# The feed-forwards' first products as seven products of quarters in a two-layer hybrid encoder

## The chip, the core and the metric

The kernel runs on one core of a Trainium2 chip. A core has five engines, each with its own queue that it works off in order: TensorE (PE, matrix products into PSUM), VectorE (DVE), ScalarE (ACT), GpSimd (POOL) and SyncE (SP, which only starts transfers here). The metric is the device time of one launch in microseconds (us).

## The reference

512 frames and 16 learned meta tokens go through a layer norm and two layers. The model has 1024 channels, a feed-forward has 2752 hidden columns in each of its two column sets.

```python
def swiglu_ffn(x, w13, w2):
    a, u = jnp.split(x @ w13, 2, axis=-1)
    return (jax.nn.silu(a) * u) @ w2
...
    for l in range(DEPTH):
        h = layer_norm(DEEPNORM_ALPHA * h + 0.5 * swiglu_ffn(h, ffn1_w13[l], ffn1_w2[l]), ln_g[l, 0], ln_b[l, 0])
        mix = token_mix(h, w_in[l], ...)
        h = layer_norm(DEEPNORM_ALPHA * h + mix, ln_g[l, 1], ln_b[l, 1])
        h = layer_norm(DEEPNORM_ALPHA * h + 0.5 * swiglu_ffn(h, ffn2_w13[l], ffn2_w2[l]), ln_g[l, 2], ln_b[l, 2])
    return h[:, N_META:]
```

`token_mix` is a projection, three groups of heads (trailing means, a depthwise convolution, chunked retention) and an output projection. All is float32.

## The kernel before

**Layout.** Activations lie transposed, channels on the 128 partitions, tokens along the columns, in 8 row tiles. The tokens are cut into two halves, s = 0 and 1, each of 256 frames and 8 meta tokens (264 columns; 256 in the last feed-forward, which drops the meta tokens). Tile m of half s is `h[m][s]`.

**Precision.** The matmuls' operands are of type float32r. Each float32 operand is split into `hi` (rounded to it, a ScalarE cast) and `lo` (the rest, a VectorE subtraction), and `mm3` makes a product of three matmuls, hi·hi, hi·lo and lo·hi, into the same PSUM bank. `xs[m][s]` is the pair for `h[m][s]`. Weights come by transfer into a raw slot of 128 x 1024 (`RAW` of them), are cast as a whole and subtracted in pieces of 512 columns into `hi` and `lo` slots (`WB` of each).

**Stages.** f0a, m0, f0b, f1a, m1, f1b: each layer l has a feed-forward a, a mixer m and a feed-forward b.

**A feed-forward** (`ffn`; the last is `last_ffn`). The hidden columns are cut into 21 units of 128 (of a and of u) and a half unit, numbered 21, with 64 of each. `PARTS` groups the units; for each part, `hidden_part` makes the hidden activations (a unit's first product by `project`: 8 row tiles times a and u times 3 matmuls for each half, `hidden` then gates and splits them), and eight steps, one for each output row tile m and each half, multiply them by `w2` (weights named `o<part>_<m>`) and add the result to h. In part 0 the first `AHEAD` = 3 units are done for half 0 first, then for half 1, since half 1's norm ends later.

**The seam to the next stage.** In the last part `normed` sets the order of the steps so that half 0 is finished first: its statistics (`center`: a mean by a matmul with ones, squares on ScalarE, a variance by a matmul, its root on VectorE, a matmul that spreads it) run beside the last `SKEW` = 6 steps of half 1, and half 1's statistics beside the next stage's first products.

**What sets the order.** The program is written as calls; a scheduler places the instructions on each engine's queue by the order of issue and the dependences, and `issue_after` holds a group back until a named instruction (`rooted["first"]` and `["second"]` are the ends of the two roots of the seam before). The kernel names 8 PSUM banks: 4 `acc`, 2 `att`, 2 `stat`.

## Time and profile before

| | before |
|---|---|
| median of 3 runs | 2049.79 us (2049.25 to 2050.43) |
| the profiled execution: own time, span | 2050.98 us, 2049.2 us |
| stages f0a, m0, f0b, f1a, m1, f1b end at | 386, 630, 1016, 1402, 1643, 2049 us |
| TensorE busy, matmuls | 98%, 15344 |
| VectorE, ScalarE, GpSimd busy | 52%, 31%, 9% |

The profile is of one execution. A row of a timeline is a start, a length and an instruction; successive rows of one engine overlap (a matmul's row of 264 columns is 0.28 us long and the next starts 0.12 us after it), so the spacing from start to start says what one costs in a run. Line numbers are those of the kernel before.

### The profile page before, as it was taken

The page shows a single profiled execution, that of the slowest core. Times are in us where ns is not written, and L with a number is a line of the kernel's source. Part 1 is how long each engine was busy: PE and PEld are TensorE (multiplying, and loading weights), DVE is VectorE, ACT ScalarE, POOL GpSimd, SP SyncE. Part 2 cuts the span into 40 slices and gives each one's busy share as a digit, 9 for nine tenths or more (in the row PEclk, how much of TensorE's full clock was granted, in tenths as well). Part 3 has the DMA queues.
Part 4 walks back from the last instruction along what each step waited for, and adds up shares of the span by engine and source line. Part 5 has one row for each costly group of instructions (what it writes and reads, how often), then busy time and mean ns, then how long its engine had stood idle before and what let it go on. Part 6 is the DMA issues. An engine that isn't in the chain of part 4 may idle for free.

```text
span 2049.2 us, 36659 instructions
## 1 busy us (share of the span) xinstructions
PE 2001.1 (98%) x15344; PEld 1924.7 (94%) x15344; DVE 1055.9 (52%) x2450; ACT 643.4 (31%) x1180; POOL 194.1 (9%) x283
## 2 busy tenths in 40 slices
...
GB/s 150 132 113 85 99 87 83 74 92 80 63 41 43 97 119 95 93 87 90 64 96 89 101 95 94 89 87 75 71 90 63 42 64 102 96 101 102 84 103 42
DMA packets 54118, 177.98 MB, mean 87 GB/s; under 512 B 6192, under 2 KB 10160, under 8 KB 53952
## 3 DMA queue, kind: packets, MB, share of 16 engines
...
q10 hardware_dynamic: 1152, 1.05, 0.2%
q14 instruction: 46, 0.38, 0.1%
...
## 4 chain that ended last, share of the span: by engine, by line
PE 84%; DVE 9%; POOL 2%; issue 2%; ACT 1%; DVEq 0%; POOLq 0%; ACTq 0%
PE f1a_y L104 2%; PE f0a_y L104 2%; PE f1a_y L105 2%; PE f1bo L764 2%; PE f1bo L766 2%; PE f0a_y L105 2%; PE f1bo L765 2%; PE f0a_y L103 2%; PE f1a_y L103 2%; PE f0b_y L104 2%; PE f0b_y L105 2%; PE f0b_y L103 2%; DVE m0y L486 1%; DVE m1y L486 1%; PE m1o L614 1%
## 5 line engine op out<-in xcount | busy, mean ns | idle before, releaser
L92 DVE TENSOR_TENSOR f1bw_l<-f1bw_r,f1bw_h 128x512 fp32r<-128x512 f32 x42 | 27.9, 685 | 48.0 <-ACT f1bw_h L89 48.0
L92 DVE TENSOR_TENSOR f0b_o_l<-f0b_o_r,f0b_o_h 128x512 fp32r<-128x512 f32 (+1 forms) x48 | 28.6, 618 | 45.1 <-ACT f0b_o_h L89 45.1
L92 DVE TENSOR_TENSOR f1a_o_l<-f1a_o_r,f1a_o_h 128x512 fp32r<-128x512 f32 (+1 forms) x48 | 28.7, 620 | 45.0 <-ACT f1a_o_h L89 45.0
L92 DVE TENSOR_TENSOR f0a_o_l<-f0a_o_r,f0a_o_h 128x512 fp32r<-128x512 f32 (+1 forms) x48 | 28.6, 618 | 44.8 <-ACT f0a_o_h L89 44.8
L486 DVE SCALAR_TENSOR_TENSOR m1y<-m1u,vec,m1y 128x528 f32<-128x528 f32 x60 | 46.7, 814 | 0.1
L486 DVE SCALAR_TENSOR_TENSOR m0y<-m0u,vec,m0y 128x528 f32<-128x528 f32 x60 | 46.6, 814 | 0.1
L89 ACT CAST f0b_o_h<-f0b_o_r 128x1024 fp32r<-128x1024 f32 (+1 forms) x24 | 22.5, 939 | 55.1 <-PE f0b_y L104 15.6
L89 ACT CAST f1a_o_h<-f1a_o_r 128x1024 fp32r<-128x1024 f32 (+1 forms) x24 | 22.5, 939 | 54.9 <-PE f1a_y L104 15.6
L89 ACT CAST f0a_o_h<-f0a_o_r 128x1024 fp32r<-128x1024 f32 (+1 forms) x24 | 22.5, 938 | 54.7 <-PE f0a_y L104 15.6
L825 POOL TENSOR_TENSOR yt<-yt,g_last 128x256 f32<-128x256 f32 x4 | 3.1, 782 | 346.8 <-ACT yt L824 346.8
L89 ACT CAST f1bw_h<-f1bw_r 128x1024 fp32r<-128x1024 f32 (+1 forms) x22 | 22.2, 1007 | 43.8 <-PE f1bo L766 6.9
L308 DVE TENSOR_TENSOR h<-h,f0b_y 128x264 f32<-128x264 f32 x32 | 13.7, 428 | 41.9 <-PE f0b_y L105 41.9
L308 DVE TENSOR_TENSOR x<-x,f0a_y 128x264 f32<-128x264 f32 x32 | 13.7, 428 | 41.7 <-PE f0a_y L105 41.6
L308 DVE TENSOR_TENSOR h<-h,f1a_y 128x264 f32<-128x264 f32 x32 | 13.7, 427 | 41.7 <-PE f1a_y L105 41.5
L251 POOL TENSOR_TENSOR f0b_ln_s<-h,h 128x264 f32<-128x264 f32 x2 | 1.5, 752 | 324.7 <-DVE h L308 324.7
L251 POOL TENSOR_TENSOR f1a_ln_s<-h,h 128x264 f32<-128x264 f32 x2 | 1.5, 754 | 324.1 <-DVE h L308 324.1
L251 POOL TENSOR_TENSOR f0a_ln_s<-x,x 128x264 f32<-128x264 f32 x2 | 1.5, 758 | 322.3 <-DVE x L308 322.3
L770 DVE TENSOR_TENSOR yt<-yt,f1bo 128x256 f32<-128x256 f32 x48 | 17.2, 417 | 24.8 <-PE f1bo L766 24.8
L104 PE MATMUL m0mo<-m0cat_l,m0wo_h 128*128 128x264 f32 x96 | 27.7, 290 | 0.0
L104 PE MATMUL m1mo<-m1cat_l,m1wo_h 128*128 128x256 f32 x96 | 27.6, 288 | 0.0
L103 PE MATMUL m0mo<-m0cat_h,m0wo_h 128*128 128x264 f32 x96 | 27.4, 288 | 0.0
L105 PE MATMUL m0mo<-m0cat_h,m0wo_l 128*128 128x264 f32 x96 | 27.3, 285 | 0.0
...
## 6 DMA issues: line engine op xcount, KB each, us to landing
f1bw_r<-in_w2last SPq DMA_DIRECT2D x20, 512.0 KB, 4.3
f0a_o_r<-in_w SPq DMA_DIRECT2D x16, 512.0 KB, 4.3
f0b_o_r<-in_w SPq DMA_DIRECT2D x16, 512.0 KB, 3.8
f1a_o_r<-in_w SPq DMA_DIRECT2D x16, 512.0 KB, 4.0
m0wo_r<-in_w_out SPq DMA_DIRECT2D x8, 512.0 KB, 3.5
m1wo_r<-in_w_out SPq DMA_DIRECT2D x8, 512.0 KB, 3.5
m0w_r<-in_w_in SPq DMA_DIRECT2D x6, 512.0 KB, 3.6
m1w_r<-in_w_in SPq DMA_DIRECT2D x6, 512.0 KB, 3.6
```

The costliest lines, as they stand in the source:

```text
L89: nc.scalar.copy(out=hi[:, :n], in_=w[:, :n])
L92: e.tensor_tensor(out=lo[:, sl], in0=w[:, sl], in1=raw(hi[:, sl]), op=ALU.subtract)
L103: nc.tensor.matmul(out, lhsT=wh, rhs=xh, start=start, stop=False)
L104: nc.tensor.matmul(out, lhsT=wh, rhs=xl, start=False, stop=False)
L105: nc.tensor.matmul(out, lhsT=wl, rhs=xh, start=False, stop=stop)
L308: nc.vector.tensor_tensor(out=y, in0=y, in1=ps, op=ALU.add)
L486: nc.vector.scalar_tensor_tensor(out=ys[c], in0=src, scalar=wk, in1=ys[c], op0=ALU.mult, op1=ALU.add)
L614: nc.tensor.matmul(o[:, c0 : c0 + cw], lhsT=v, rhs=sm, start=i == 0, stop=i == len(sms) - 1)
L764: nc.tensor.matmul(o, lhsT=hh, rhs=wh, start=part > 0 and i == 0, stop=False)
L765: nc.tensor.matmul(o, lhsT=hh, rhs=wl, start=False, stop=False)
L766: nc.tensor.matmul(o, lhsT=hl, rhs=wh, start=False, stop=i == nk - 1)
L770: nc.vector.tensor_tensor(out=y[:, :256], in0=y[:, :256], in1=o, op=ALU.add)
```

## The change

Units 0, 1 and 21 of each feed-forward are made as before. For each of the other 19, the two column sets of a unit (a, u), the two halves of the rows of the weights (row tiles 0 to 3 and 4 to 7) and the two halves of the tokens form a 2 x 2 by 2 x 2 block product. It is made with Winograd's form of Strassen's method: seven products of quarters in place of eight, of sums of the operands.

- `sums`, once in a feed-forward, makes s1 to s4 of `h` (16 sums on VectorE) and splits them (16 casts, 16 subtractions) into wide slots.
- `sum_weights`, for each unit, makes t1 to t4 out of the raw weights, in place, and splits them: on VectorE four sums and seven subtractions of 512 columns, on ScalarE two casts of 1024 and three of 512.
- `hidden_by_sums` issues the products in the order P, R, P, Q, P, Q, P, where P, Q and R are banks. A bank is added to over several products; between them ScalarE copies what it holds (m1, u2, m5, u3), and VectorE forms a and u of both halves of the tokens from the copies.
- Five parts in place of three, four to five units each. `RAW` is 4 in place of 3, `WB` 5 in place of 7, `hc` (the ring of split hidden tiles) 20 in place of 32. `SKEW_F` = 8 holds for the seams behind feed-forwards: all steps of half 0 come before any of half 1.
- A pool of 16 wide slots of 558 columns holds what had slots of its own: the tokens at the start, sequences and windows of the mixer, its last split heads, the last `w2` and `w_out` weights (`weights_wide`), and the split sums.
- The norm behind the mixer keeps h for all tiles, which `sums` needs.

```diff
-TILES = {"x": 32, "h": 16, "hc": 32, "g": 4, "r2": 2, "sm": 5, "s": 2, "q": 4, "dg": 2}
+TILES = {"x": 32, "h": 16, "hc": 20, "g": 4, "r2": 2, "sm": 5, "s": 2, "q": 4, "dg": 2}
+WIDE, WIDES = 558, 16
 BANKS = {"acc": 4, "att": 2, "stat": 2}
-RAW, WB = 3, 7
-SKEW, AHEAD = 6, 3
+RAW, WB, YB = 4, 5, 2
+SKEW, SKEW_F, AHEAD = 6, 8, 3
 
...
-PARTS = ([0, 1, 21, 2, 3, 4], list(range(5, 13)), list(range(13, 21)))
+PARTS = ([0, 1, 21, 2, 3], *(list(range(u, u + 4)) for u in (4, 8, 12)), list(range(16, 21)))
...
+    def wide(name, dt=F32):
+        return sq_pool.tile([P, WIDE], dt, tag="wide", name=name, bufs=WIDES)
...
-    def normed(n, step, ns, v, name, keep):
+    def normed(n, step, ns, v, name, keep, skew):
 
         for s in range(2):
-            for m in range(n - SKEW):
+            for m in range(n - skew):
                 step(m, s)
-        for m in range(n - SKEW, n):
+        for m in range(n - skew, n):
             step(m, 0)
...
+    def sums(n, name):
+        out = [[], [], [], []]
+        for i in range(KT // 2):
+            (a11, a21), (a12, a22) = ([y[:, :n] for y in h[m]] for m in (i, i + KT // 2))
+            s1, s2, s3, s4 = (t(f"{name}s{j}{i}", "q" if i % 2 else "sm")[:, :n] for j in range(4))
+            nc.vector.tensor_tensor(out=s1, in0=a21, in1=a22, op=ALU.subtract)
+            nc.vector.tensor_tensor(out=s2, in0=s1, in1=a11, op=ALU.subtract)
+            nc.vector.tensor_tensor(out=s3, in0=a11, in1=a21, op=ALU.subtract)
+            nc.vector.tensor_tensor(out=s4, in0=a12, in1=s2, op=ALU.add)
+            for j, y in enumerate((s1, s2, s3, s4)):
+                out[j].append(split_wide(y, n, f"{name}S{j}{i}"))
+        return out
+    def half_split(w, hi, lo, c):
+        sl = slice(c, c + 512)
+        nc.scalar.copy(out=hi[:, sl], in_=w)
+        nc.vector.tensor_tensor(out=lo[:, sl], in0=w, in1=raw(hi[:, sl]), op=ALU.subtract)
+    def sum_weights(src, name):
+        def pair(k, w=1024, b=WB):
+            return [wp.tile([P, w], F32R, tag=f"{p_}{'' if w == 1024 else w}", name=f"{name}{k}_{p_}", bufs=b) for p_ in ("hi", "lo")]
+        wa, wu = (wp.tile([P, 1024], F32, tag="raw", name=f"{name}{b}_r", bufs=RAW) for b in "au")
+        nc.sync.dma_start(out=wa, in_=src[0])
+        nc.sync.dma_start(out=wu, in_=src[1])
+        b11, b21, b12, b22 = wa[:, :512], wa[:, 512:], wu[:, :512], wu[:, 512:]
+        add = lambda o, y: nc.vector.tensor_tensor(out=o, in0=o, in1=y, op=ALU.add)
+        A, X, U, Y = pair("a"), pair("x"), pair("u"), pair("y", 512, YB)
+        nc.scalar.copy(out=A[0], in_=wa)
+        for c in (0, 512):
+            nc.vector.tensor_tensor(out=A[1][:, c : c + 512], in0=wa[:, c : c + 512], in1=raw(A[0][:, c : c + 512]), op=ALU.subtract)
+        add(b11, b12)
+        half_split(b11, *X, 0)
+        add(b12, b22)
+        nc.scalar.copy(out=U[0], in_=wu)
+        add(b11, b22)
+        half_split(b11, *X, 512)
+        for c in (0, 512):
+            nc.vector.tensor_tensor(out=U[1][:, c : c + 512], in0=wu[:, c : c + 512], in1=raw(U[0][:, c : c + 512]), op=ALU.subtract)
+        add(b21, b11)
+        half_split(b21, *Y, 0)
+        return [at(w, slice(c, c + 512)) for w, c in ((A, 0), (A, 512), (X, 0), (X, 512), (U, 0), (U, 512), (Y, 0))]
+    def hidden_by_sums(w, S, n, name):
+        b11, b21, t1, t2, t3, b22, t4 = w
+        s1, s2, s3, s4 = S
+        a11, a12, a22 = ([xs[m][s] for m in range(k, k + KT // 2)] for k, s in ((0, 0), (KT // 2, 0), (KT // 2, 1)))
+        p_, q_, r_ = acc(f"{name}P"), acc(f"{name}Q"), acc(f"{name}R", "att")
+        def product(o, x, w, first):
+            for i in range(KT // 2):
+                mm3(o[:, :n], at(w, slice(i * P, (i + 1) * P)), at(x[i], slice(0, n)), first and i == 0, i == KT // 2 - 1, True)
+        def copy(o, k):
+            y = t(f"{name}{k}", "sm")[:, :n]
+            nc.scalar.copy(out=y, in_=o[:, :n])
+            return y
+        def gated(g, u, s):
+            nc.vector.scalar_tensor_tensor(out=g, in0=u, scalar=0.5, in1=g, op0=ALU.mult, op1=ALU.mult)
+            return split(g, n, f"{name}x{s}")
+        product(p_, a11, b11, True)
+        m1 = copy(p_, "m1")
+        product(r_, a12, b21, True)
+        nc.vector.tensor_tensor(out=m1, in0=r_[:, :n], in1=m1, op=ALU.add)
+        g0 = t(f"{name}g0", "g")[:, :n]
+        nc.scalar.activation(g0, m1, AF.Silu)
+        product(p_, s2, t2, False)
+        u2 = copy(p_, "u2")
+        product(q_, s1, t1, True)
+        m5 = copy(q_, "m5")
+        product(p_, s3, t3, False)
+        u3 = copy(p_, "u3")
+        nc.vector.tensor_tensor(out=m5, in0=m5, in1=u3, op=ALU.subtract)
+        product(q_, s4, b22, False)
+        nc.vector.tensor_tensor(out=u2, in0=q_[:, :n], in1=u2, op=ALU.subtract)
+        first = gated(g0, u2, 0)
+        product(p_, a22, t4, False)
+        g1 = t(f"{name}g1", "g")[:, :n]
+        nc.scalar.activation(g1, p_[:, :n], AF.Silu)
+        return [first, gated(g1, m5, 1)]
+    summed = {}
     def hidden_part(part, src, ns, name, between={}):
         hid, w = {}, {}
-        for u, s in in_two(PARTS[part], AHEAD if part == 0 else 0, between):
+        plain = PARTS[part][: AHEAD if part == 0 else 0]
+        for u, s in in_two(plain, AHEAD, between):
             if s == 0:
-                i = PARTS[part].index(u)
-                late = part == 0 and "first" in rooted and i >= LATE_W
+                i = plain.index(u)
+                late = "first" in rooted and i >= LATE_W
                 with tc.issue_after(rooted["second" if i >= LATE_B else "first"]) if late else nullcontext():
                     w[u] = unit_weights(u, src, f"{name}_{u}")
                 hid[u] = []
             hid[u].append(hidden(u, w[u], s, ns[s], f"{name}_{u}"))
+        if part == 0:
+            summed[name] = sums(ns[0], name)
+        for u in PARTS[part][len(plain) :]:
+            with tc.issue_after(rooted["second"]) if plain and "second" in rooted else nullcontext():
+                wu = sum_weights(src["p"][u], f"{name}_{u}")
+            hid[u] = hidden_by_sums(wu, summed[name], ns[0], f"{name}_{u}")
         return hid
...
-                    w[m] = weights(w2[m, :, full[0] * P : (full[0] + nk) * P], nk * P, f"{name}_o{part}_{m}")
+                    make = weights_wide if part == len(PARTS) - 1 and m >= KT - 3 else weights
+                    w[m] = make(w2[m, :, full[0] * P : (full[0] + nk) * P], nk * P, f"{name}_o{part}_{m}")
...
-                normed(KT, step, ns, v, f"{name}_ln", i == 1)
+                normed(KT, step, ns, v, f"{name}_ln", i == 1, SKEW_F)
...
-                w[m] = weights(a["w_out"][l, m], 1024, f"{name}wo{m}")
+                w[m] = (weights_wide if m >= KT - 2 else weights)(a["w_out"][l, m], 1024, f"{name}wo{m}")
...
-        normed(KT, step, no, V_LN + (3 * l + 1) * 16, f"{name}_ln", not last)
+        normed(KT, step, no, V_LN + (3 * l + 1) * 16, f"{name}_ln", True, SKEW)
```

Three places show how the instructions stand.

VectorE's queue in f1a, from the last of the splits of the sums to the first product of unit 2 (`f1aS` is a split sum, `f1a_2a_lo` and `f1a_2x_lo` are subtractions for unit 2's weights, line 427 its sums of weights, `f1a_21h` the gate of the half unit, `f1a_2m` what comes out of unit 2's first two banks). After the change:

```order
L127 TENSOR_TENSOR f1aS_13084<-f1as_13070,f1aS_13084 128x264 [waits Activation_49]
L390 SCALAR_TENSOR_TENSOR f1a_21h_12998<-f1a_21p_0_12972,f1a_21g_12997 64x264 [waits PE_49,Activation_49]
L390 SCALAR_TENSOR_TENSOR f1a_21h_12998<-f1a_21p_0_12972,f1a_21g_12997 64x264
L431 TENSOR_TENSOR f1a_2a_lo<-f1a_2a_r,f1a_2a_hi 128x512 [waits DMAHW2_49]
L117 TENSOR_TENSOR f1a_21x_l<-f1a_21h_12998,f1a_21x_h 128x264 [waits Activation_49]
L431 TENSOR_TENSOR f1a_2a_lo<-f1a_2a_r,f1a_2a_hi 128x512
L427 TENSOR_TENSOR f1a_2a_r<-f1a_2a_r,f1a_2u_r 128x512 [waits DMAHW3_49,DVE_49]
L427 TENSOR_TENSOR f1a_2u_r<-f1a_2u_r 128x512 [waits DVE_49]
L416 TENSOR_TENSOR f1a_2x_lo<-f1a_2a_r,f1a_2x_hi 128x512 [waits Activation_49]
L468 TENSOR_TENSOR f1a_2m_13130<-f1a_2R,f1a_2m_13130 128x264 [waits PE_49]
```

Before, the same gate of the half unit stands behind unit 2's weights and the last split of the norm:

```order
L92 TENSOR_TENSOR f1a_2u_l<-f1a_2u_r,f1a_2u_h 128x512 [waits DMAHW1_49]
L92 TENSOR_TENSOR f1a_2u_l<-f1a_2u_r,f1a_2u_h 128x512
L291 TENSOR_TENSOR f0b_ln_x6l<-h_1_7281,f0b_ln_x6h 128x264 [waits Activation_49]
L363 SCALAR_TENSOR_TENSOR f1a_21h_11921<-f1a_21p_0_11895,f1a_21g_11920 64x264 [waits PE_49,Activation_49]
L363 SCALAR_TENSOR_TENSOR f1a_21h_11921<-f1a_21p_0_11895,f1a_21g_11920 64x264
L98 TENSOR_TENSOR f1a_21x_l<-f1a_21h_11921,f1a_21x_h 128x264 [waits Activation_49]
```

The weights of unit 2, which stood ahead of the half unit's gate, now stand behind it and behind all sums.

ScalarE's queue in f1a, in the middle of part 1 (line 458 copies a bank, 415 casts a sum of weights, 429 and 435 cast raw weights, 470 is a silu). After the change:

```order
L458 COPY f1a_4m_13722<-f1a_4P 128x264 [waits PE_49]
L415 CAST f1a_5x_hi<-f1a_5a_r 128x512 [waits DVE_49]
L435 CAST f1a_5u_hi<-f1a_5u_r 128x1024 [waits DVE_49,DMAHW3_49,PE_49,Activation_49]
L470 ACTIVATE f1a_4g_13737<-f1a_4m_13722 128x264 [waits DVE_49]
L458 COPY f1a_4u_13751<-f1a_4P 128x264 [waits PE_49]
L415 CAST f1a_5x_hi<-f1a_5a_r 128x512 [waits DVE_49]
L429 CAST f1a_6a_hi<-f1a_6a_r 128x1024 [waits DMAHW4_49,PE_49,Activation_49]
L458 COPY f1a_4m_13765<-f1a_4Q 128x264 [waits PE_49]
L458 COPY f1a_4u_13779<-f1a_4P 128x264 [waits PE_49]
```

Before, at the same place:

```order
L368 ACTIVATE f1a_5g_12895<-f1a_5p_0_12845 128x264 [waits PE_49]
L97 CAST f1a_5x_h<-f1a_5g_12895 128x264 [waits DVE_49]
L89 CAST f1a_8u_h<-f1a_8u_r 128x1024 [waits DMAHW7_49,PE_49,Activation_49]
L368 ACTIVATE f1a_5g_12952<-f1a_5p_0_12902 128x264 [waits PE_49]
L89 CAST f1a_9a_h<-f1a_9a_r 128x1024 [waits DMAHW0_49,PE_49,Activation_49]
L97 CAST f1a_5x_h<-f1a_5g_12952 128x264 [waits DVE_49]
```

Between two reads of PSUM there stood at most one cast of weights; now the copies of a unit's banks stand among up to two, one of them waiting for VectorE, and weights are made one to two units ahead instead of three to four.

ScalarE's queue at the seam from f0b to f1a (line 291, before 264, is the square of a centred tile; `f1a_0a`, `f1a_0u` are the next stage's first weights). After the change:

```order
L116 CAST f0b_20x_h<-f0b_20g_12108 128x264 [waits DVE_49]
L104 CAST f0b_o_7_h_12295<-f0b_o_7_r 128x128
L291 ACTIVATE f0b_ln_q_12327<-h_0_7236 128x264 [waits DVE_49]
L91 CAST f1a_0a_h<-f1a_0a_r 128x1024 [waits DMAHW5_49,PE_49]
L291 ACTIVATE f0b_ln_q_12330<-h_0_7271 128x264 [waits DVE_49]
L291 ACTIVATE f0b_ln_q_12334<-h_0_7340 128x264 [waits DVE_49]
```

Before:

```order
L97 CAST f0b_20x_h<-f0b_20g_11045 128x264 [waits DVE_49]
L89 CAST f0b_o_7_h<-f0b_o_7_r 128x1024 [waits DMAHW2_49,PE_49]
L89 CAST f1a_0a_h<-f1a_0a_r 128x1024 [waits DMAHW3_49,PE_49]
L264 ACTIVATE f0b_ln_q_11379<-h_0_6775 128x264 [waits DVE_49]
L264 ACTIVATE f0b_ln_q_11382<-h_0_6810 128x264 [waits DVE_49]
```

The cast of `f1a_0a`, which stood ahead of the first square, stands between the first and the second.

## Rows read from the trace of the kernel before

**Rows 1.** The page: span, busy time by engine, the chain that ended last.
```profile
span 2049.2 us, 36659 instructions
PE 2001.1 (98%) x15344; PEld 1924.7 (94%) x15344; DVE 1055.9 (52%) x2450; ACT 643.4 (31%) x1180; POOL 194.1 (9%) x283
...
PE 84%; DVE 9%; POOL 2%; issue 2%; ACT 1%; DVEq 0%; POOLq 0%; ACTq 0%
```

**Rows 2.** Windows: length, busy us of each engine, PEclk, DMA share, GB/s.
```profile
752.00:860.00 108.00, 108.00 (x887) 108.00 (x886) 39.19 (x77) 30.53 (x52) 0.00 (x0) 1.00 0.32 95
860.00:915.00 55.00, 55.00 (x453) 55.00 (x452) 17.83 (x34) 10.51 (x14) 0.00 (x0) 1.00 0.30 87
1016.00:1402.00 386.00, 383.08 (x3128) 381.08 (x3126) 164.85 (x348) 117.79 (x207) 20.98 (x26) 1.00 0.31 89
```

**Rows 3.** TensorE's waits at the seam f0b to f1a: total us, times, longest.
```profile
PE f0b_ln_rs L159 <- DVE f0b_ln_q L271: 1.0, 1, 1.0
...
PE f1a_0p L104 <- DVE f0b_ln_x6l L291: 0.8, 1, 0.8
...
PE f0b_ln_rs L171 <- DVE f0b_ln_dg L162: 0.4, 1, 0.4
...
PE f0b_ln_mean L256 <- DVE f0b_ln_s L254: 0.3, 1, 0.3
PE f1a_0p L104 <- DVE f0b_ln_x4l L291: 0.3, 1, 0.3
```

**Rows 4.** TensorE's timeline, first and last of 96 matmuls, f0b and f1b.
```profile
798.32 0.28 PE L103 MATMUL f0b_9p<-m_ln_x0h,f0b_9a_h 128*128 128x264 f32 x1
...
809.92 0.28 PE L105 MATMUL f0b_9p<-m_ln_x7h,f0b_9u_l 128*128 128x264 f32 x1
...
1811.35 0.28 PE L103 MATMUL f1b_9p<-m_ln_x0h,f1b_9a_h 128*128 128x256 f32 x1
...
1822.51 0.28 PE L105 MATMUL f1b_9p<-m_ln_x7h,f1b_9u_l 128*128 128x256 f32 x1
```

**Rows 5.** TensorE's timeline at the seam f0b to f1a.
```profile
1016.40 0.71 PE L256 MATMUL f0b_ln_mean<-f0b_ln_s,ones 128*128 128x264 f32 x2
...
1036.21 0.28 PE L103 MATMUL f1a_0p<-f0b_ln_x0h,f1a_0a_h 128*128 128x264 f32 x1
...
1059.66 0.39 PE L104 MATMUL f1a_0p<-f0b_ln_x6l,f1a_0a_h 128*128 128x264 f32 x1 [0.77 <-DVE f0b_ln_x6l L291]
```

**Rows 6.** VectorE's timeline: weights of unit 6; the seam f0b to f1a.
```profile
739.96 1.29 DVE L92 TENSOR_TENSOR f0b_6a_l<-f0b_6a_r,f0b_6a_h 128x512 fp32r<-128x512 f32 x2 [0.33 <-ACT f0b_6a_h L89]
...
1033.42 0.43 DVE L291 TENSOR_TENSOR f0b_ln_x0l<-h,f0b_ln_x0h 128x264 fp32r<-128x264 f32 x1
...
1038.80 2.81 DVE L262 TENSOR_TENSOR h<-h,f0b_ln_mean 128x264 f32<-128x264 f32 x8 [0.81 <-PE f0b_ln_mean L256]
...
1049.33 2.08 DVE L281 SCALAR_TENSOR_TENSOR h<-h,vec,f0b_ln_rs 128x264 f32<-128x264 f32 x5
...
1058.63 0.97 DVE L291 TENSOR_TENSOR f0b_ln_x6l<-h,f0b_ln_x6h 128x264 fp32r<-128x264 f32 x1
1059.63 0.88 DVE L363 SCALAR_TENSOR_TENSOR f1a_21h<-f1a_21p,f1a_21g 64x264 f32<-64x264 f32 x2
```

**Rows 7.** ScalarE's timeline in f0b: weight casts, a silu, a cast.
```profile
774.61 1.05 ACT L89 CAST f0b_9u_h<-f0b_9u_r 128x1024 fp32r<-128x1024 f32 x1 [4.48 <-PE f0b_6p L104]
775.57 0.38 ACT L368 ACTIVATE f0b_6g<-f0b_6p 128x264 f32<-128x264 f32 x1
775.85 1.04 ACT L89 CAST f0b_10a_h<-f0b_10a_r 128x1024 fp32r<-128x1024 f32 x1
776.79 0.41 ACT L97 CAST f0b_6x_h<-f0b_6g 128x264 fp32r<-128x264 f32 x1
```

**Rows 8.** The page's DMA issues: count, KB each, us to landing.
```profile
f1a_o_r<-in_w SPq DMA_DIRECT2D x16, 512.0 KB, 4.0
```

More of the change, by code (lines that the diff above doesn't have):

```diff
@@ L93, in weights, with weights_wide, tile_of @@
         return hi, lo
+    def weights_wide(src, n, name):
+        w = wp.tile([P, 1024], F32, tag="raw", name=f"{name}_r", bufs=RAW)
+        nc.sync.dma_start(out=w[:, :n], in_=src)
+        out = []
+        for c in range(0, n, 512):
+            k = min(512, n - c)
+            hi, lo = (wide(f"{name}_{p_}{c}", F32R) for p_ in "hl")
+            nc.scalar.copy(out=hi[:, :k], in_=w[:, c : c + k])
+            nc.vector.tensor_tensor(out=lo[:, :k], in0=w[:, c : c + k], in1=raw(hi[:, :k]), op=ALU.subtract)
+            out.append((hi, lo))
+        return out
+    def tile_of(w, j):
+        if isinstance(w, list):
+            return at(w[j // 4], slice(j % 4 * P, (j % 4 + 1) * P))
+        return at(w, slice(j * P, (j + 1) * P))
     def split(src, n, name, tag="hc"):
```

52 lines of the change are left out of this document (28 added, 24 removed).

## The prediction, made before the changed kernel was run

> **What bounds the kernel now.** The page comes first. TensorE is busy 98% of the span and the chain that ended last runs 84% on it [rows 1]: VectorE at 52% and ScalarE at 31% are covered. The shares are averages, so the stages come next. The windows [rows 2] show a whole feed-forward (1016 to 1402 us) with TensorE at 383.08 of 386 us and full clock; a stretch of first products alone (752 to 860) and one of second products alone (860 to 915) have TensorE busy all the time, VectorE 36% and 32%, ScalarE 28% and 19%. In the list of TensorE's waits every one of a feed-forward lies at its seam to the next stage; the five of the seam from f0b to f1a [rows 3] add up to 2.8 us. So inside a feed-forward the time is the number of matmuls times their spacing, and what is taken from that number comes off the time as long as nobody else is late.
>
> **What the change removes.** A unit of 128 hidden columns costs 96 matmuls for both halves before (2 halves, 2 column sets, 8 row tiles, 3 matmuls) and 84 after (7 products, 4 row tiles, 3 matmuls). Units 0, 1 and the half unit 21 stay plain, so 19 units in each of four feed-forwards lose 12 matmuls: 684 of 264 columns in three of them, 228 of 256 columns in the last. Their spacing is read from start to start over one half of unit 9 [rows 4]: (809.92 − 798.32)/95 = 122.1 ns at 264 columns, (1822.51 − 1811.35)/95 = 117.5 ns at 256. 684 × 0.1221 + 228 × 0.1175 = 83.5 + 26.8 = **110.3 us off**. The second products keep their matmuls; five parts in place of three only group them differently.
> The Trainium skill ("TensorE: Matmul & The Clock Gate", section "Back-to-back issue gap") gives columns/2.4 GHz + 2.5 ns for the gap of warm matmuls, 112.5 and 109.2 ns here, with which the gain would be 101.8 us; it speaks of an isolated gap. The rows include the weight load of each matmul, and the measurement decides.
>
> **What it adds off the path.** Prices from rows: a 512-column VectorE pass 0.61 us apiece in a run ([rows 6], two in 1.29 with an overlap), a 264-column pass 0.35 (eight in 2.81), a 1024-column ScalarE cast 1.05, a 264-column pass out of PSUM 0.38, a cast of 264 0.41 [rows 7]; a 512-column cast is not in the rows, between the last two by length 0.62 (estimate). A sum unit needs on VectorE 11 passes of 512 and 7 of 264 (before 4 and 4): 11 × 0.61 + 7 × 0.35 = 9.2 us. On ScalarE two casts of 1024, three of 512, four copies out of PSUM, two silus, two casts of 264: 2.1 + 1.9 + 1.5 + 0.8 + 0.8 = 7.1 us. TensorE's unit is 84 × 0.122 = 10.25 us. Both fit, VectorE with 1 us to spare. A part's second product (8 steps of two halves, 24 matmuls, 23 us) asks VectorE for about 16 × 0.35 + 8 × 0.61 = 11 us, so a backlog of a part is worked off there. The cover is thus thin but closed, and I price the averages at nothing; without it each microsecond of VectorE over 10.25 in a unit costs 76 us. SyncE's queue moves the same bytes through four raw slots instead of three: a unit's two transfers wait for the last pass over the unit two ahead, land 4.0 us later [rows 8] and have a whole unit's 10.25 us for it: nothing, unless VectorE is over 6 us late. The other edits (wide slots for tokens, mixer sequences and some weights, h kept by the mixer norm) fall where [rows 1] show VectorE half idle: nothing, ±3 us.
>
> **What it adds on the path.**
> *(a) The first sum unit of each feed-forward.* Its operands are sums over h of both halves, so it needs the second half's norm in full. At the seam the spread of the second half starts on VectorE at Z = 1049.33 [rows 6], and TensorE, after waiting for the last lo tile (x6l), resumes at 1059.66 = Z + 10.3 [rows 5]. About 80 plain matmuls are left there by the order, so they end at Z + 10.3 + 9.8 = Z + 20.1. VectorE has from x6l on 16 sums and 16 splits, 32 × 0.35 = 11.2 us, 12 with a few waits for casts: Z + 22.4. The first place shown from the order says what stands behind them in VectorE's queue: the two gates of the half unit (0.88 us [rows 6]) and a 512 pass of unit 2's weights (0.62), and only then can the first lo matmul run; four hi matmuls (0.5 us) can run ahead. That is 22.4 + 1.5 − 0.5 − 20.1 = 3.3 us of stall. The unit's other weights are made behind it, at 0.61 us a pass and some products need two or three passes while the one before lasts 1.46: I put 0.4 for t1, 1.2 for t2, 0.5 for the next unit's first piece, 2 us. And the part's first second-product weights wait for a raw slot that unit 3 frees only with its last pass, and then stand on ScalarE ahead of a bank copy: about 2 us. Together 7 us for three feed-forwards, 5 for the first (its second half enters early): **26**, bounds 8 (2 each, part of the 3.3 alone) and 50 (VectorE 12 us late each time, as if nothing of the sums were covered).
> *(b) The seams.* The feed-forward norms now do all eight steps of the first half before any of the second. Between the first half's mean and the next stage's first use lie 1036.21 − 1016.40 = 19.8 us now [rows 5], and the chain of that norm ends with x0l on VectorE at 1033.42 + 0.43 [rows 6], 17.4 us after the mean. After the change the order has 111 matmuls there, 13.6 us, and 0.85 for the statistics' own matmuls: 14.4 us. ScalarE's queue (the third place) has a 1024 cast of the next stage's weights between the first two squares of the chain, where it stood ahead of both. So the chain comes out about 3 us late, where the first half waits 1.0 + 0.4 us on the variance and its root today [rows 3]: about 2 us more at three seams, **6**, bounds 0 (VectorE freer, chain 14 us) and 15.
> *(c) Bank handshakes.* No row of before shows a bank read while the next product waits to go on in it. Here ScalarE copies m1, u2, m5 and u3 out of two banks, and TensorE is back in a bank after one other product, 12 × 0.122 = 1.46 us. A copy (0.38) fits, and one that stands right behind a 1024 cast (1.05 + 0.38 = 1.43, the second place shown) just about. 45 of the 76 copies of m5 stand so. I take 0.1 us for each of these: **5**, bounds 0 and 25 (the copy a whole 0.38 late with a hand-over as long as the 0.3 to 0.4 us waits in [rows 3]).
> *(d) Into each second product*, the last unit's lo split is about 0.35 us late, some 16 times: **5**, bounds 0 and 10.
>
> **Sum.** The profiled execution took 2050.98 us, 1.2 above the median of the runs. 2050.98 − 110.3 + 26 + 6 + 5 + 5 = 1982.7, less 1.2: **1981 us**.
>
> **The rivals.**
> *Everything hidden.* The sums start as the spread goes and the handshakes all fit; then 2050 − 110 plus 1 to 15 us, about **1945**. For it: ScalarE 30% and VectorE 43% busy over the feed-forward [rows 2]. Against it: the 12 us of sums have one engine and stand in one place of its queue.
> *Banks decide.* Each unit loses about 0.7 us because two of the four copies stand behind a cast that itself waits for data: 76 × 0.7 = 53 us more than full gain on top of (a) and (b), about **2030**. For it: casts in the order wait for a DMA and for VectorE, and everything behind waits too. Against it: they are made a unit ahead. The Trainium skill ("PSUM — Partial Sum Buffer", section "🎯 Summary: rules for kernel authors") says to read PSUM beside a running matmul only in another bank and to guard by bank, so each of these waits is unavoidable; no run here shows yet what one costs.
> *VectorE becomes the bound, slower.* A unit saves 12 × 0.122 = 1.46 us. If VectorE, with its waits for TensorE and ScalarE inside the unit, takes over 10.25 + 1.46 = 11.7 us for it instead of 9.2, the change loses on each of 76 units; at 12.5 us it is (12.5 − 11.7) × 76 = 61 us slower, less what second products work off, plus (a) and (b): about **2100**. For it: 18 passes in strict order, most of which wait for a cast of ScalarE or for a product. Against it: weights are made a unit ahead, and when VectorE is late its waits vanish, so it goes back to 9.2.
> *No change:* losses of about 110 us, an accident between the last two.
>
> **How the numbers follow.** Forecast (1958 to 2008) 0.60; everything hidden 0.13; banks decide (2008 to 2045) 0.16; no change 0.03; slower 0.08. Within 0.2%, about 4 us, a measurement of this kernel can't tell from no change. Faster is 0.60 + 0.13 + 0.16 = 0.89, same 0.03, slower 0.08. The range leaves out the lower half of the second case, the upper half of the third, and the last two, about 0.2: 1948 to 2022.
>
> **What would show it.** TensorE's instructions about 14,420 instead of 15,344, with spacing unchanged in a sum unit. (a): a TensorE wait of about 3 us on VectorE's unit-2 weights in each feed-forward, then one on o0_1. (b): the waits on x0l and the variance grow at three seams. (c): waits of 0.1 to 0.2 us on the copies, in about half of the units. VectorE busy near 1580 us; inside a hidden stretch near 90%. The prediction is wrong if TensorE's waits in the middle of parts (units 5 to 20) sum to much over 15 us, or if the first sum unit starts without a stall.

## The result, and the profile after

The changed kernel takes 1979.93 us (median of 4 runs, 1979.15 to 1982.23), the kernel before 2049.52 on the same chip (2048.08 to 2050.43): a ratio of 0.9663, with an interval of 0.9646 to 0.968. It is 3.4% faster. The forecast was 1981 us, with 1948 to 2022 as the range.

The page of the changed kernel answers to [rows 1]:

```profile
span 1977.5 us, 36739 instructions
...
PE 1912.4 (97%) x14423; PEld 1826.3 (92%) x14423; DVE 1548.9 (78%) x3466; ACT 920.1 (47%) x1845; POOL 215.0 (11%) x283
...
PE 79%; DVE 12%; POOL 3%; issue 3%; ACT 2%; DMA 0%; SPq 0%; DVEq 0%; POOLq 0%; ACTq 0%
```

TensorE has 921 instructions fewer (912 of them in the units) and is still busy nearly all the time, although VectorE went from 52% to 78%. The chain that ended last has more of VectorE in it (12% after 9%): somewhere it now sets the time. The windows say where not. The first is the whole of f1a, the second its units 4 to 7, the third the second product behind them (columns as in [rows 2]):

```profile
997.47:1366.78 369.31, 361.27 (x2897) 356.29 (x2897) 288.33 (x603) 186.47 (x376) 24.93 (x32) 1.00 0.30 94
1085.74:1126.95 41.21, 41.21 (x338) 41.03 (x337) 33.09 (x64) 24.15 (x49) 0.00 (x0) 1.00 0.32 98
1126.95:1150.63 23.68, 23.68 (x194) 23.53 (x193) 17.44 (x36) 7.79 (x12) 0.00 (x0) 1.00 0.34 102
```

Inside a part TensorE is never without work: it is busy 41.21 of 41.21 us, with VectorE at 80% and ScalarE at 59% beside it. But f1a as a whole has 8.0 us in which TensorE is not busy, where it had 2.9 before in [rows 2]. The list of TensorE's waits for that stretch, from its last norm matmuls on (total us, times, longest), shows one that is new:

```profile
PE f1a_2P L135 <- DVE f1a_2a_lo L431: 2.5, 1, 2.5
PE f0b_ln_rs L201 <- DVE f0b_ln_dg L192: 0.7, 1, 0.7
PE f1a_0p L133 <- ACT f0b_ln_x0h L315: 0.4, 1, 0.4
```

It is the first sum unit. The other feed-forwards have it too: 1.1 us in f0a and 2.8 in f0b on the same subtraction, and 3.1 in f1b on ScalarE's cast of that unit's sum of weights.

The balance of the two profiled executions: the span fell by 2049.2 − 1977.5 = 71.7 us, and 684 matmuls of 122.1 ns and 228 of 117.5 ns are worth 110.3, so 38.6 us were given back (the medians are 69.6 us apart, so single executions leave some 2 us open):

| where | predicted, us | found, us |
|---|---|---|
| (a) start of the sums, four times | 26 | 22.2 (25.6 against the same parts without sums) |
| (b) seams, three | 6 | 6.5 |
| (c) hand-overs of banks | 5 | 6.6 |
| (d) into and in the second products | 5 | 3.6 |
| end: last matmul to the end, 17.86 after 13.38 | 0 (± 3) | 4.5 |
| the two mixers | 0 | −5.6 |

(a) is read as the time from a feed-forward's first matmul to its first second product, four stages, with the 24 matmuls of units 2 and 3 that the sums save put back; (b) as the time from a norm's mean to the next stage's first use, less the matmuls that lie there; (c) as the length of units 4 to 20, 68 of them, against 84 spacings (10.22 us, in f1b 9.92). The lines add up to 37.8, and 0.8 stays unassigned.

### The profile page after: what moved, and what is told of

Its sections match the earlier page's. It is cut to its first block, busy times and chain, and to the rows that moved or that the text cites. A ratio compares the mean times of both kernels' runs of the same rounds, so it can differ in the third digit from the quotient of the medians.

```text
span 1977.5 us, 36739 instructions
## 1 busy us (share of the span) xinstructions
PE 1912.4 (97%) x14423; PEld 1826.3 (92%) x14423; DVE 1548.9 (78%) x3466; ACT 920.1 (47%) x1845; POOL 215.0 (11%) x283
## 4 chain that ended last, share of the span: by engine, by line
PE 79%; DVE 12%; POOL 3%; issue 3%; ACT 2%; DMA 0%; SPq 0%; DVEq 0%; POOLq 0%; ACTq 0%
PE f0a_y L134 2%; PE f0a_y L133 2%; PE f1bo L890 2%; PE f1bo L888 2%; PE f0a_y L135 2%; PE f1bo L889 2%; PE f0b_y L134 2%; PE f1a_y L134 2%; PE f0b_y L133 2%; PE f0b_y L135 2%; PE f1a_y L135 2%; PE f1a_y L133 2%; DVE m0y L610 1%; DVE m1y L610 1%; PE m0sc L719 1%
## 5 line engine op out<-in xcount | busy, mean ns | idle before, releaser
L91 ACT CAST f0a_o_h<-f0a_o_r 128x512 fp32r<-128x512 f32 (+1 forms) x37 | 23.5, 635 | 48.4 <-PE f0a_y L134 29.5
L91 ACT CAST f1a_o_h<-f1a_o_r 128x512 fp32r<-128x512 f32 (+1 forms) x37 | 23.6, 637 | 48.0 <-PE f1a_y L134 29.0
L91 ACT CAST f0b_o_h<-f0b_o_r 128x512 fp32r<-128x512 f32 (+1 forms) x37 | 23.5, 636 | 47.6 <-PE f0b_y L134 29.3
L335 DVE TENSOR_TENSOR x<-x,f0a_y 128x264 f32<-128x264 f32 x64 | 27.1, 425 | 23.3 <-PE f0a_y L135 23.1
L335 DVE TENSOR_TENSOR h<-h,f0b_y 128x264 f32<-128x264 f32 x64 | 27.1, 425 | 23.2 <-PE f0b_y L135 23.1
L335 DVE TENSOR_TENSOR h<-h,f1a_y 128x264 f32<-128x264 f32 x64 | 27.1, 424 | 23.1 <-PE f1a_y L135 23.0
L91 ACT CAST f1bw_h<-f1bw_r 128x1024 fp32r<-128x1024 f32 (+1 forms) x22 | 22.2, 1011 | 21.0 <-PE f1bo L890 4.2
L894 DVE TENSOR_TENSOR yt<-yt,f1bo 128x256 f32<-128x256 f32 x80 | 27.8, 414 | 5.4 <-PE f1bo L890 5.3
L291 ACT ACTIVATE m_ln_q<-h 128x264 f32<-128x264 f32 (+1 forms) x32 | 11.9, 414 | 39.7 <-DVE h L289 36.1
L257 PE MATMUL tr<-ident,xtok 128*128 128x128 f32 (+1 forms) x48 | 10.9, 328 | 12.1 <-DVE xtok L242 11.4
L281 POOL TENSOR_TENSOR m_ln_s<-m_ln_s,h 128x264 f32<-128x264 f32 (+1 forms) x20 | 18.2, 912 | 32.0 <-DVE h L329 26.1
L257 PEld LDWEIGHTS tr<-ident,xtok 128*128 128x128 f32 (+1 forms) x48 | 6.8, 167 | 16.1 <-issue 14.8
```

The lines of the kernel that those rows point to most:

```text
L91: nc.scalar.copy(out=hi[:, :n], in_=w[:, :n])
L335: nc.vector.tensor_tensor(out=y, in0=y, in1=ps, op=ALU.add)
L894: nc.vector.tensor_tensor(out=y[:, :256], in0=y[:, :256], in1=o, op=ALU.add)
```

## The experiments

**Five parts and wide slots alone.** All units plain:

```diff
-        plain = PARTS[part][: AHEAD if part == 0 else 0]
+        plain = PARTS[part]
...
-        if part == 0:
-            summed[name] = sums(ns[0], name)
```

> All units are made plain again (eight products, 96 matmuls a unit, no sums); the five parts, the wide slots, the slot counts and SKEW_F = 8 stay as changed. Theory: of the 72 us by which the changed kernel's span is shorter, the matmuls give 110 and are charged 19 by the wait at the first sum unit of each feed-forward (with the slow clock behind it) and 7 by the bank hand-overs; so without the sums the kernel takes 1980 + 110 - 26 = 2064 us, and its seams behind feed-forwards and its end stay as long as in the changed kernel (17.9 us from the last matmul to the end). Rival: five parts and wide slots cost nothing by themselves and all the missing gain belongs to the sums: 2050 us or less.

Measured: 2056.10 us, before beside it 2048.25, ratio 1.0039 (1.0024 to 1.0054). That is 0.4% slower than before, but 8 us below what I had expected: the sums' own losses are 34 us (110.3 less the 76.0 between the spans), not 26. The frame, that is everything but the sums, costs 4.3 us between the two profiled executions and 7.9 between the medians. Its end alone loses 4.4 (17.74 us from the last matmul on). The three seams lose 7.6, and the mixers (4.7) and the four starts (3.4) give about as much back. Of this, 5.0 us lie in m1: TensorE's wait at its first scores is 1.4 us shorter, and the lower clock behind it lasts 3.4 us instead of 10.2, in this kernel and in the changed one.

**Unit 2 plain too.** The sums start with unit 3; 12 matmuls more in each feed-forward, and 11.7 us more of plain work under which the sums are made:

```diff
-        plain = PARTS[part][: AHEAD if part == 0 else 0]
+        plain = PARTS[part][: AHEAD + 1 if part == 0 else 0]
```

> Unit 2 of each feed-forward is made plain, ahead of the first sum unit (3), so 18 units are made by sums: 48 matmuls more, 5.8 us. Theory: the start of the sums waits for VectorE's queue, and another 10 us of plain matmuls cover it: the waits at the first sum unit (5 us in f0b, f1a, f1b each with the slow clock behind them, 3 in f0a) go, minus 19, so about 13 us faster, 1967 us. Rival: VectorE stays behind until the first part ends, and the wait only moves to unit 3 and its second product: 1980 to 1986 us.

Measured: 1963.84 us, ratio 0.9587 (0.9573 to 0.9601). It makes 48 matmuls more and is 16 us faster. TensorE's waits from the seam to behind the first sum unit of f1a, in full, have nothing of that unit any more (in f0a and f1b a wait of 0.8 and 0.9 us is left at unit 3):

```profile
PE f0b_ln_rs L201 <- DVE f0b_ln_dg L192: 0.7, 1, 0.7
PE f1a_0p L133 <- ACT f0b_ln_x0h L315: 0.4, 1, 0.4
PE f1a_0p L134 <- DVE f0b_ln_x4l L318: 0.4, 2, 0.2
PE f1a_1p L133 <- DVE h L335: 0.4, 1, 0.4
PE f1a_0p L134 <- DVE f0b_ln_x6l L318: 0.3, 1, 0.3
```

The four stretches from a stage's start to its first second product are 15.3 us shorter together (233.8 for 249.2), so the gain lies where (a) put the loss.

**Norms behind feed-forwards as before.**

```diff
-SKEW, SKEW_F, AHEAD = 6, 8, 3
+SKEW, SKEW_F, AHEAD = 6, 6, 3
```

> The seams behind the feed-forwards keep 6 steps of the second half behind the first half's statistics, as before, in place of 8. Theory: the first half's chain is what the seam waits for, and its cover falls by 30 matmuls, 3.7 us, at three seams; with the slow clock that may follow a wait of that length (1.5 us) 11 to 16 us slower, about 1993 us. Rival: the chain is not the bound (VectorE's queue is): within 3 us of 1980.

Measured: 1978.95 us, ratio 0.9669 (0.9653 to 0.9685): no change. TensorE's waits at the same seam are 1.9 us at the variance's sum and 1.1 at x0h, where the changed kernel has 1.8, 0.4 and another 0.7 at the root, so about the same in sum:

```profile
PE f0b_ln_rs L189 <- DVE f0b_ln_q L298: 1.9, 1, 1.9
PE f1a_0p L133 <- ACT f0b_ln_x0h L315: 1.1, 1, 1.1
```

This edit takes 30 matmuls, 3.7 us, from the cover of the first half's chain, and the next stage's first use comes 3.5 us sooner, 15.07 us after the mean for 18.54. TensorE's timeline has mean, spread and first use, in the changed kernel and here:

```profile
978.93 0.71 PE L283 MATMUL f0b_ln_mean<-f0b_ln_s,ones 128*128 128x264 f32 x2
995.63 0.71 PE L201 MATMUL f0b_ln_rs<-f0b_ln_dg,ones 88*128 88x264 f32 x2 [0.67 <-DVE f0b_ln_dg L192]
997.47 0.39 PE L133 MATMUL f1a_0p<-f0b_ln_x0h,f1a_0a_h 128*128 128x264 f32 x1 [0.40 <-ACT f0b_ln_x0h L315]
```

```profile
979.90 0.71 PE L283 MATMUL f0b_ln_mean<-f0b_ln_s,ones 128*128 128x264 f32 x2
993.13 0.71 PE L201 MATMUL f0b_ln_rs<-f0b_ln_dg,ones 88*128 88x264 f32 x2
994.97 0.39 PE L133 MATMUL f1a_0p<-f0b_ln_x0h,f1a_0a_h 128*128 128x264 f32 x1 [1.13 <-ACT f0b_ln_x0h L315]
```

So the chain has no fixed length: with less cover it is shorter. Its spread comes 13.23 us after the mean for 16.70, with four of VectorE's weight passes ahead of it instead of eight. A shorter cover is thus not by itself what (b) costs.

**A bank of its own for the product that goes back to Q.** The product of s4 and b22 goes into a fourth bank, and VectorE adds what the bank added:

```diff
+        z_ = acc(f"{name}Z", "att")
...
+        nc.vector.tensor_tensor(out=u2, in0=m5, in1=u2, op=ALU.subtract)
-        product(q_, s4, b22, False)
-        nc.vector.tensor_tensor(out=u2, in0=q_[:, :n], in1=u2, op=ALU.subtract)
+        product(z_, s4, b22, True)
+        nc.vector.tensor_tensor(out=u2, in0=z_[:, :n], in1=u2, op=ALU.add)
```

> The product s4 x b22 gets a bank of its own instead of going on in Q, so TensorE has no more to wait until ScalarE has copied m5 out of Q; VectorE adds the two instead, one pass of 264 columns more a unit (9.5 us of VectorE in a unit of 10.2). Theory: the 0.10 to 0.16 us in front of that product in about 60 of 76 units is the wait for the copy, and goes: 7 us faster, 1973 us, every unit from 4 on at 10.22 us (9.9 in f1b). Rival: VectorE has no time to give, and the added pass makes later units wait: no change or up to 10 us slower.

Measured: 1973.10 us, ratio 0.9632 (0.9618 to 0.9647), as the theory of the hand-over said. In the changed kernel ScalarE's timeline of unit 5 (start, length) has the copy of m5 right behind a cast of 1024 columns:

```profile
1102.09 1.05 ACT L429 CAST f1a_7a_hi<-f1a_7a_r 128x1024 fp32r<-128x1024 f32 x1 [0.24 <-ACT f1a_6y_hi L415]
1103.04 0.37 ACT L458 COPY f1a_5m<-f1a_5Q 128x264 f32<-128x264 f32 x1
```

and TensorE's timeline, at the return to Q,

```profile
1103.18 0.28 PE L134 MATMUL f1a_5P<-f1aS,f1a_5u_hi 128*128 128x264 f32 x1
1103.30 0.28 PE L135 MATMUL f1a_5P<-f1aS,f1a_5u_lo 128*128 128x264 f32 x1
1103.46 0.39 PE L133 MATMUL f1a_5Q<-f1aS,f1a_5u_hi 128*128 128x264 f32 x1
1103.69 0.28 PE L134 MATMUL f1a_5Q<-f1aS,f1a_5u_hi 128*128 128x264 f32 x1
```

goes on after 0.16 and 0.23 us instead of twice 0.12: 0.15 us lost, of which only 0.04 is the wait and 0.11 the longer step from the matmul behind it to the next. With a bank of its own, at the same place:

```profile
1099.20 0.28 PE L135 MATMUL f1a_5P<-f1aS,f1a_5u_lo 128*128 128x264 f32 x1
1099.32 0.28 PE L133 MATMUL f1a_5Z<-f1aS,f1a_5u_hi 128*128 128x264 f32 x1
1099.44 0.28 PE L134 MATMUL f1a_5Z<-f1aS,f1a_5u_hi 128*128 128x264 f32 x1
```

**Four units in the last part.**

```diff
-PARTS = ([0, 1, 21, 2, 3], *(list(range(u, u + 4)) for u in (4, 8, 12)), list(range(16, 21)))
+PARTS = ([0, 1, 21, 2, 3], list(range(4, 8)), list(range(8, 12)), list(range(12, 17)), list(range(17, 21)))
```

> Units 12 to 16 form the fourth part and 17 to 20 the last, so the last part has four units instead of five: steps of 12 matmuls at the seams, 2.9 us less cover behind the first half's mean, and 2.8 instead of 3.5 us for each token tile at the end. First theory of the seam (a chain of fixed length against a cover that has shrunk): 3 us more at each of three seams, and 2 us more at the end since VectorE's about 5 us of work for a token tile have less beside them: 11 to 14 us slower, about 1992 us. Second theory, since 6 steps of cover in place of 8 changed nothing: the seam's loss does not hang on the length of the cover, only the end is longer: 2 to 4 us slower, about 1983 us.

Measured: 1989.52 us, ratio 0.9714 (0.97 to 0.9729), 9.6 slower than the changed kernel, which is neither theory's number. The end takes 20.57 us, 2.7 more, and each seam's uncovered time is 7.4 to 8.0, about 2.2 more, while the first half's chain is no later. Units 8, 5 and 4 in the last part thus go with ends of 13.38, 17.86 and 20.57 us, which fits that less second product is left under which the first token tiles can be finished; the next run tests it.

**The last second product in another order.** In the last part of the last feed-forward, token tiles are finished one after another, (tile, column half) = (0,0), (1,0), (0,1), (1,1), (2,0), (2,1), (3,0), (3,1), with the second column half's weights in wide slots:

```diff
+            if part == len(PARTS) - 1:
+                w, ps = [[], []], {}
...
+                for tt, ch in ((0, 0), (1, 0), (0, 1), (1, 1), (2, 0), (2, 1), (3, 0), (3, 1)):
```

> Only the order of the last part of the last feed-forward is changed: the two output column halves of a token tile are made one behind the other (tiles 0 and 1 of the first half of the columns, then of the second, then tile 2 whole, then tile 3 whole), and the weights of the second half lie in wide slots. Theory: the 17.9 us from the last matmul to the end (13.4 before) are a backlog of VectorE, which has about 5 us of work for a token tile while the five-unit part feeds it one each 3.5 us; with 7 us between the last two tiles there is no backlog, and the end is back at 13 us: 4 us faster, 1976 us. Rival: the end is a chain of the last tile alone, or the second half's weights come late into the slots that the split sums leave: no gain or a few us slower.

Measured: 1974.68 us, ratio 0.9642 (0.9627 to 0.9658). The windows from the last matmul to the end, before, after and here:

```profile
2035.82:2049.20 13.38, 0.28 (x3) 0.07 (x1) 9.60 (x34) 1.41 (x3) 3.84 (x5) 0.67 0.29 98
```

```profile
1959.64:1977.50 17.86, 0.29 (x3) 0.08 (x1) 14.38 (x48) 3.60 (x7) 8.49 (x11) 0.61 0.26 88
```

```profile
1958.42:1971.70 13.28, 0.28 (x3) 0.07 (x1) 9.69 (x39) 1.42 (x3) 3.06 (x4) 0.63 0.28 97
```

VectorE's 14.38 us behind the last matmul are back at 9.69, and the time is 5.3 us shorter.

**Half of the sums' splits on GpSimd.** `split_wide` takes an engine, and the subtractions for s1 and s3 go to GpSimd:

```diff
-                out[j].append(split_wide(y, n, f"{name}S{j}{i}"))
+                out[j].append(split_wide(y, n, f"{name}S{j}{i}", nc.gpsimd if j in (0, 2) else nc.vector))
```

> Eight of the 16 subtractions that split the sums (those of s1 and s3) are made on GpSimd instead of VectorE; nothing is left out. Theory: the first sum unit waits for VectorE's queue, so 8 x 0.35 = 2.8 us less in it take 2.5 us of wait away in each of four feed-forwards, and the slow clock behind it: 10 to 14 us faster, about 1968 us. Rival: GpSimd, at about 0.75 us a pass and behind the odd tiles of the norm, is late itself, or slows VectorE while both run: no gain.

Measured: 1985.35 us, ratio 0.9688 (0.9671 to 0.9704): no gain, but 5 us lost. In f1a the wait for unit 2's first subtraction is gone, and two others stand a few matmuls behind it:

```profile
PE f1a_2Q L133 <- ACT f1a_2x_hi L415: 1.2, 1, 1.2
PE f1a_2Q L135 <- DVE f1a_2x_lo L416: 1.2, 1, 1.2
```

They are for the cast and the subtraction of that unit's sum of weights; no wait of TensorE is put down to a GpSimd pass on the sums. Those passes (least, median and longest in ns) are

```profile
L127 POOL TENSOR_TENSOR f1aS<-f1as,f1aS x8: 754/949/4132, 1025.3 to 1038.4; 128x264 fp32r<-128x264 f32 x8
```

and in the other three feed-forwards 0.72 to 1.04 us each. While GpSimd works, some of VectorE's own passes are longer, and these include the ones that unit 2's weights need:

```profile
1036.61 1.25 DVE L431 TENSOR_TENSOR f1a_2a_lo<-f1a_2a_r,f1a_2a_hi 128x512 fp32r<-128x512 f32 x1
1037.78 0.98 DVE L117 TENSOR_TENSOR f1a_1x_l<-f1a_1g,f1a_1x_h 128x264 fp32r<-128x264 f32 x1
1038.68 1.24 DVE L427 TENSOR_TENSOR f1a_2a_r<-f1a_2a_r,f1a_2u_r 128x512 f32<-128x512 f32 x1
1039.95 0.69 DVE L427 TENSOR_TENSOR f1a_2u_r<-f1a_2u_r 128x512 f32<-128x512 f32 x1
```

The start of f1a to its first second product is 59.95 us for 60.25, that of f1b 66.83 for 65.82, and all four together are 1.7 us longer. So the stall only moves, and most of the 5 us lies elsewhere: in the profiled execution the lower clock behind seams and m1's scores takes some 3 us more, and the first matmul comes 1.5 us later. Whether the edit brings these is not shown.

**Three edits together**: unit 2 plain, the bank of its own, the last product's order.

> Three edits together: unit 2 plain, a bank of its own for s4 x b22, and the last part's order of the tail run. If the three costs are separate, the gains add: 16 for the plain unit, 7 for the bank, 4 for the tail: 1980 - 27 = 1953 us. If VectorE is short of time in the hidden stretches with the added pass, or the costs cover each other, less: 1956 to 1963 us.

Measured: 1954.21 us (1953.66 to 1955.34), ratio 0.9538 (0.9524 to 0.9552), 25.7 faster than the changed kernel; the three alone gave 16.1, 6.8 and 5.3, 28.2 in sum. So the three costs are separate but for some 2.5 us. This is the fastest version.

**Weights at a seam one unit later**, to take the passes over unit 1's weights out of VectorE's queue ahead of the spread:

```diff
-LATE, LATE_W, LATE_B = 3, 2, 2
+LATE, LATE_W, LATE_B = 3, 1, 2
```

> One number: LATE_W is 1 instead of 2, so the weights of the second unit of a stage (unit 1) are held back until the root of the first half's norm is made. Third theory of the seam, since neither fewer steps of cover (no change) nor a smaller last part (a third of what was reckoned) followed the first two: the first half's chain is as long as VectorE's queue makes it, and in the changed kernel eight weight passes of 0.61 us stand between its variance and its spread. At the seam f0b to f1a four of them leave: the spread comes 14.3 us after the mean instead of 16.7, and the seam's uncovered time falls from 5.0 us to about 2.8. The seams behind the mixers change too, by up to 1 us either way; f0a and the seams into the mixers do not. In sum 1 to 4 us faster, 1976 to 1979 us. Rival: the passes are only wanted a little later and TensorE waits for them instead: no change, or 1 to 3 us slower.

Measured: 1986.09 us, ratio 0.9691 (0.9678 to 0.9705), 6 slower. The spread comes 14.78 us after the mean instead of 16.70, as reckoned, but the next stage's first use moves only from 18.54 to 18.00, and the waits move behind it. TensorE's waits at the seam now have x4l and x7l at 1.0 and 1.4:

```profile
PE f1a_0p L134 <- POOL f0b_ln_x7l L313: 1.4, 1, 1.4
PE f1a_0p L134 <- DVE f0b_ln_x4l L318: 1.0, 1, 1.0
```

These two explain about 2 us of the loss. In the profiled execution 5.9 us more lie in f1b's transposes and the second product behind them, where the granted clock was 0.51 over 10.2 us (from 1667.0 on), behind waits of only 0.3 and 0.4 us. Whether the edit has to do with that is not shown.

**The same on top of the three.**

> The three edits that gained (unit 2 plain, a bank of its own, the tail's order, 1954 us together) with LATE_W = 1 as the fourth. If the later weights help by themselves they help here alike: 1951 to 1953 us. If they are waited for: 1954 to 1957 us.

Measured: 1959.53 us, ratio 0.9559 (0.9546 to 0.9572), 5 slower than the three alone. The waits on x7l and x4l at the seam from f0b to f1a, 1.4 and 1.0 us, stand there with unit 2 plain as well.

**Empty matmuls into the first sum unit's wait.** 16 matmuls into a bank that nobody reads, at the place where TensorE waits:

```diff
+            if part == 0 and u == PARTS[0][len(plain)]:
+                fill = stat(f"{name}_fill")
+                for _ in range(16):
+                    nc.tensor.matmul(fill[:, : ns[0]], lhsT=ident_r, rhs=xs[0][0][0][:, : ns[0]], start=True, stop=True)
```

> The changed kernel with 16 matmuls of 264 columns more in each feed-forward, ahead of the first sum unit, into a bank that nobody reads (the output is unchanged). They take 16 x 0.122 = 2.0 us and stand where TensorE waits 2.5 to 3.1 us for VectorE in f0b, f1a and f1b (1.1 in f0a). Theory: the wait itself costs nothing more by being filled, and the granted clock, which fell to 0.5 for about 3.4 us behind it, stays at 1.0: 1.4 to 2.0 us less at three places and 1 us more in f0a: 3 to 5 us faster, 1976 us. Rival: the clock falls for another reason, or the matmuls come too late and are added: 0 to 8 us slower.

Measured: 1979.44 us (1975.41 to 1981.05), ratio 0.9653 (0.964 to 0.9667): in the time, inconclusive. In the place it did what it should. The changed kernel's windows over the wait and behind it, then this kernel's behind it:

```profile
1031.80:1034.90 3.10, 0.58 (x5) 0.41 (x4) 3.02 (x8) 1.15 (x4) 0.00 (x0) 1.00 0.00 0
1034.90:1038.40 3.50, 3.50 (x19) 3.50 (x19) 2.46 (x4) 1.69 (x3) 0.00 (x0) 0.52 0.02 5
```

```profile
1034.50:1038.00 3.50, 2.92 (x24) 2.71 (x23) 3.25 (x6) 1.24 (x4) 0.00 (x0) 1.00 0.00 0
...
378.60:382.10 3.50, 3.50 (x17) 3.50 (x17) 2.27 (x7) 0.00 (x0) 0.25 (x1) 0.50 0.49 139
```

The granted clock stays at 1.00, where it had fallen to 0.52, and the first second product comes 0.8 to 1.1 us sooner in three of four feed-forwards. The last line is another place of this execution, a seam whose wait was followed by the slower clock; such stretches at its three seams cost it 2.6, 1.4 and 1.5 us, while the changed kernel's profiled execution has one of 1.5 us. In that execution this outweighs the gain at the starts, 2.8 us over the four.

## Why the prediction was right

The gross gain held: 14,423 instructions of TensorE (some 14,420 predicted), a unit of 10.22 us inside the parts where no hand-over is late (10.25 predicted). VectorE was priced at 1580 us and has 1549, 80% in a hidden stretch where 90 were said. It never became the bound inside a part, so the rival on the slower side fell, and "banks decide" with it: a hand-over loses 0.15 us, not 0.7 a unit.

Two readings of the prediction were wrong without changing its sum. The two windows that it calls first products alone and second products alone hold both kinds: the second product of that part runs from 845.22 to 892.12 us. Taken there, VectorE is busy 34% in first products (751.41 to 845.22) and 40% in second ones, instead of 36% and 32%. And the chances outside its range add up to 0.25, not 0.2.

**(a)** is the largest loss and was sized right, 22 to 26 us for 26, and unit 2 as plain work takes most of it away (by the same reckoning 4.5 of 25.6 are left). Its make-up was half wrong, so that the size came out is in part luck. The stall is there with its reason: VectorE's queue in f1a has the last split of the sums, the half unit's gates and only then unit 2's first subtraction, as the order had shown:

```profile
1031.34 1.46 DVE L127 TENSOR_TENSOR f1aS<-f1as,f1aS 128x264 fp32r<-128x264 f32 x4
1032.83 0.88 DVE L390 SCALAR_TENSOR_TENSOR f1a_21h<-f1a_21p,f1a_21g 64x264 f32<-64x264 f32 x2
1033.74 0.69 DVE L431 TENSOR_TENSOR f1a_2a_lo<-f1a_2a_r,f1a_2a_hi 128x512 fp32r<-128x512 f32 x1
```

TensorE's timeline waits for that last line 2.52 us, of 3.3 predicted:

```profile
1031.68 0.28 PE L134 MATMUL f1a_2R<-f0b_ln_x4l,f1a_2a_hi 128*128 128x264 f32 x1
1034.49 0.39 PE L135 MATMUL f1a_2P<-f0b_ln_x0h,f1a_2a_lo 128*128 128x264 f32 x1 [2.52 <-DVE f1a_2a_lo L431]
...
1035.31 0.42 PE L134 MATMUL f1a_2P<-f0b_ln_x2l,f1a_2a_hi 128*128 128x264 f32 x1
1035.53 0.42 PE L135 MATMUL f1a_2P<-f0b_ln_x2h,f1a_2a_lo 128*128 128x264 f32 x1
```

But the 2 us that the prediction put on the first second-product weights (`o0_1`) did not occur. In its place stands what the last two rows show: the matmuls behind the stall come every 0.22 us instead of 0.12, at a granted clock of 0.52 over the window, the lower level of 1.2 GHz, for some 3.4 us in f0b and f1a and for 6 us in f1b. That costs 1.4, 1.5 and 2.1 us there in this execution. The first of the three is partly chance: four other runs have the same wait of 2.8 us in f0b, and the clock stays at 1.00 behind it.

**(b)** has the right size, 6.5 us for 6, by a wrong step. The prediction took a chain of fixed length (17.4 us after the mean) against a cover that falls from 135 to 111 matmuls, because the last part has five units in place of eight. But with 81 matmuls of cover, `SKEW_F` = 6, the seam costs the same, since the chain shortens with the cover. And the cast of the next stage's weights between the first two squares, which the prediction named, costs nothing up to the variance: the chain from the mean to the variance takes 9.1 us before and after (8.6 with four units in the last part). TensorE arrives earlier at the variance, and waits 1.8 us there for 1.0 before, and VectorE's weight passes of 0.61 us (eight in the changed kernel from the mean to the spread, six before) stand ahead of the spread, which comes 16.70 us after the mean for 14.26. Taking some of those out brought the spread forward, as reckoned, but not the time: the waits came back behind it. What sets the whole 2.2 us of each seam stays open in part.

**(c)** was sized right for the reason given: 6.6 us for 5. 28 of 51 units in f0a, f0b and f1a lose 0.09 to 0.18 us, and in f1b all 17 do (10.07 us in the mean, 9.93 with a bank of its own): 45 of 68 units, where the prediction had counted 45 of 76 from the order. Behind the product Z these losses are all gone, so the prediction was wrong to call such waits unavoidable under "Banks decide".

**(d)** came out at 3.6 us, as a spacing of 122 to 125 ns in the second products of the first three feed-forwards where 121 to 122 stood before; no single wait carries it, and its cause stays open.

**Missed both ways.** The prediction put the other edits at nothing, ± 3 us. The end lost 4.5, since the last part has five units in place of eight, and the mixers gained 5.6. These two cancel, and so the total is nearer than its parts. Why the second mixer gained is not tested further: TensorE's wait at its first scores is 3.5 us on GpSimd instead of 4.9 on VectorE, and the stretch at the lower clock behind it is 3.4 us instead of 10.2, with the sums or without.
